# A head's output squared in PSUM and scaled on its way out by ScalarE, in a one-core hybrid encoder layer

## The chip, the cores and the metric

One core of one Trainium2 chip runs the whole layer in one launch. The metric is the device time of that launch in microseconds (us). The kernel before takes 1037.61 us, the median of 3 runs (1036.9 to 1039.13).

## The reference

The layer has 512 tokens of width 1024. One projection of x gives the inputs of two branches and two gates; the part that matters here is the branch of gated delta rules, with 8 heads of width 128 and a forward and a backward pass.

```python
proj = x @ w_in[l]
qkv, z, a, bb, sc_b, sc_c, sc_x, gate_a, gate_b = _split_in(proj)
...
o = o_fwd + o_bwd
zf = z.astype(jnp.float32).reshape(bsz, t, N_HEADS, HEAD_DIM)
o = (o * lax.rsqrt(jnp.mean(jnp.square(o), axis=-1, keepdims=True) + RMS_EPS)
     * norm_w.astype(jnp.float32) * jax.nn.silu(zf))
return o.reshape(bsz, t, GDN_WIDTH).astype(out_dtype) @ w_o
...
mixed = jax.nn.sigmoid(gate_a) * y_a + jax.nn.sigmoid(gate_b) * y_b
x = _layer_norm(DEEPNORM_ALPHA * x + mixed @ w_out[l], ln1_g[l], ln1_b[l])
h = jnp.square(jax.nn.relu(x @ w_up[l] + b_up[l]))
x = _layer_norm(DEEPNORM_ALPHA * x + h @ w_down[l] + b_down[l], ln2_g[l], ln2_b[l])
```

The change is in the middle statement: for each head and token, the sum of squares of the output o, the inverse root of it, and the product of o with that root.

## The kernel before

All large products run in three passes: each float32 operand is split into a high part, made by a ScalarE copy, and a low part, made by a VectorE subtraction (`split`, `split_w`), and TensorE adds high times high, high times low and low times high (lines 158 to 160). A block of projection is 8 steps (`KT`) of three 128x512 matmuls, in `proj_steps`; its weights come by DMA, are split some steps ahead, and stand in two buffers.

The heads' own work is small against that and is woven into the stream of projection blocks. Nine slots (`h` from 0 to 8, line 777) each run some blocks; a slot has `L` steps, 8 times the number of its blocks. By `REST` and the three blocks of the next head's keys, queries and values, slots 1 to 5 have 48 steps, slots 6 and 7 have 40, and slot 8 has 8. At each step `u` of slot `h` up to three generators are advanced by one piece: `new`, the local part of head h + 1; `mid`, the rest of the local part of head h, which inverts a triangular matrix by blocks; and `far`, the scan over chunks and the end of head h - 1. Tables say at which steps: `FAR` for `far`, `MID` for `mid`, `BEGIN` for `new`.

```python
for _ in range(FAR.count(u) if far else 0):
    step(far)
...
for g in (mid, far) if h < NH else ():
    if g:
        run(g)
```

An entry of a table that is not below the slot's `L` is never met in the loop; what is left of `mid` and then of `far` is run at once when the slot is over (the second loop above, line 801). Inside these slots the order written here is the order of the instructions on TensorE, VectorE, ScalarE and GpSimd (`manual_schedule`), and each engine takes its list in order. The last head's `far` runs on beside the next stage's blocks (line 820 and after), every third step.

The scan (`gdn_scan`) adds both directions of a head's output into one PSUM bank, `po`, tag "o", of which there is one buffer; the next head's scan writes the same bank. At the scan's end, ScalarE copies `po` (128 tokens x 4 chunks x 128) to `ot` in SBUF (line 687). Then `gdn_end` has three pieces. In the first ScalarE squares `ot` chunk by chunk and sums each token's row into `so` (line 695). In the second VectorE and GpSimd make the inverse root `ro` of `so` by three Newton steps (`rsqrt`, whose tile is `nryo`; it ends with line 425), and GpSimd multiplies `ot` by it (line 699). In the third TensorE transposes the four chunks into `pot` (line 703) and ScalarE copies that to `on`, scaled by the norm's weight (line 704).

Other names: `pyb` is the last product of the block inversion in `mid` (line 615), which VectorE (line 619) and ScalarE (line 621) copy into `na`; `dg` (line 507) and `vt` (line 526) are copies of `new`; `kd` (line 650) is a 128x128 copy from SBUF scaled by token, `vh` (line 668) a 128x128 copy from PSUM; `px`, `lx` and `py` (lines 574 to 583) are an earlier step of the inversion; `wh_in` (line 124) is the high part of a block's weights, `ps_in` and `ps_osc` are banks of projection blocks.

Of the kernel before, what the change touches and what calls it, by code (L numbers as in the profile page):

```python
# [8 lines left out]
F32 = mybir.dt.float32  # L9
F32R = mybir.dt.float32r  # L10
I32 = mybir.dt.int32
AF = mybir.ActivationFunctionType
ALU = mybir.AluOpType
AX = mybir.AxisListType

P = 128
# [4 lines left out]
NCH = 4  # L21
# [18 lines left out]
KEYS1 = 31  # L40
MID = (0, 2, 15, 19, 24, 25, 27, 29, 30, 33, 36, 40)
MID0 = (23, 23, 34, 49, 56, 56, 58, 59, 60, 64, 70, 92)
FAR = (0, 4, 8, 10, 13, 13, 14, 14, 14, 14, 15, 15, 20, 25, 30, 31, 48)
SPLIT_AT = (3, 2)
LOW_AFTER = (3, 5)
CONV = ((0, 1, 3), (0, 1, 3), (0, 0, 3), (5, 3, 4))
# [15 lines left out]
def kernel(  # L62
# [25 lines left out]
    nc = tc.nc  # L88
    act = nc.scalar.activation
# [11 lines left out]
    def ps(kind, name, shape=(P, NT)):  # L101
        return psum.tile(list(shape), F32, tag=kind, name=name, bufs={"m": 2, "g": 2, "l": 1, "s": 2, "o": 1}[kind])
# [143 lines left out]
    gdn = tc.alloc_tile_pool(name="gdn", bufs=1, side="right")  # L246
# [49 lines left out]
    for d in range(2):  # L296
        stt(out=gg[:, d], in0=pl[:, :, 8 * d:8 * d + 8], scalar=-1.0,
            in1=ea[:, 8 * d:8 * d + 8].unsqueeze(1).broadcast_to([P, NCH, 8]), op0=ALU.mult, op1=ALU.mult)
# [47 lines left out]
    for g in range(2):  # L346
        for t in range(2):
            nc.sync.dma_start(out=eye.rearrange("(b g) (s t) j -> g t b s j", g=2, t=2)[g, t],
                              in_=diag[2 * t + g, 0:4, 0:16].partition_broadcast(P // 2))
# [63 lines left out]
    def rsqrt(v, name):  # L413

        eng = nc.gpsimd if RS_POOL else nc.vector
        y = gdn.tile([P, NCH], F32, tag=f"nry{name[0]}", name=f"nry{name}", bufs=2)
        t = gdn.tile([P, NCH], F32, tag=f"nrt{name[0]}", name=f"nrt{name}", bufs=2)
        nc.vector.tensor_scalar(out=t.bitcast(I32), in0=v.bitcast(I32), scalar1=1, scalar2=None, op0=ALU.logical_shift_right)
        nc.vector.tensor_scalar(out=y.bitcast(I32), in0=t.bitcast(I32), scalar1=-1.0, scalar2=float(0x5F3759DF),
                                op0=ALU.mult, op1=ALU.add)  # L420
        for _ in range(3):
            eng.tensor_tensor(out=t, in0=y, in1=y, op=ALU.mult)
            eng.tensor_tensor(out=t, in0=t, in1=v, op=ALU.mult)
            eng.tensor_scalar(out=t, in0=t, scalar1=-0.5, scalar2=1.5, op0=ALU.mult, op1=ALU.add)
            eng.tensor_tensor(out=y, in0=t, in1=y, op=ALU.mult)
        return y
# [213 lines left out]
    def gdn_scan(h, qk, kt, vt, W, AT, qd, nbk, ss):  # L640
        po = ps("o", f"po{h}")
        S = [None, None]
        first = True
        for i in range(NCH):
            chunk = (i, NCH - 1 - i)
            kds = []
            if i != NCH - 1:
                for d, c in enumerate(chunk):
                    kd = gdn.tile([P, P], F32, tag="kd", name=f"kd{h}_{d}_{c}", bufs=4)
                    act(out=kd, in_=kt[:, c, :], func=AF.Copy, scale=nbk[:, d, c:c + 1])  # L650
                    kds.append(kd)
                yield
            pcs, vhs, Rs = [], [], []
            for d, c in enumerate(chunk):
                pcs.append(ps("s", f"pc{h}_{d}_{c}"))
                Rs.append(vt[:, c, :])
            if i:
                for d, c in enumerate(chunk):
                    nc.tensor.matmul(pcs[d][:, 0:P], qk[:, 0, c * P:(c + 1) * P], S[d], start=True, stop=True)
                    Rs[d] = gdn.tile([P, P], F32, tag="R", name=f"R{h}_{d}_{c}", bufs=2)  # L660
                    stt(out=Rs[d], in0=pcs[d][:, 0:P], scalar=egc[:, d, c, h:h + 1], in1=vt[:, c, :], op0=ALU.mult, op1=ALU.add)
                for d, c in enumerate(chunk):
                    nc.tensor.matmul(po[:, c * P:(c + 1) * P], qd[:, d, c, :], S[d], start=False, stop=False, skip_group_check=True)
                yield
            for d, c in enumerate(chunk):
                nc.tensor.matmul(pcs[d][:, P:2 * P], W[:, d, c, :], Rs[d], start=True, stop=True)  # L666
                vh = gdn.tile([P, P], F32, tag="vh", name=f"vh{h}_{d}_{c}", bufs=4)
                act(out=vh, in_=pcs[d][:, P:2 * P], func=AF.Copy)
                vhs.append(vh)
            yield  # L670
            if i != NCH - 1:
                for d, c in enumerate(chunk):
                    ds = pcs[d][:, 2 * P:3 * P]
                    nc.tensor.matmul(ds, kds[d], vhs[d], start=True, stop=True)
                    Sn = gdn.tile([P, P], F32, tag="S", name=f"S{h}_{d}_{c}", bufs=4)
                    if i == 0:
                        act(out=Sn, in_=ds, func=AF.Copy)
                    else:
                        stt(out=Sn, in0=S[d], scalar=egl[:, d, c, h:h + 1], in1=ds, op0=ALU.mult, op1=ALU.add)
                    S[d] = Sn  # L680
            for d, c in enumerate(chunk):
                nc.tensor.matmul(po[:, c * P:(c + 1) * P], AT[:, d, c, :], vhs[d], start=first, stop=False, skip_group_check=True)
                first = False
            if i != NCH - 1:
                yield
        ot = gdn.tile([P, NCH, P], F32, tag="ot", name=f"ot{h}", bufs=1)
        act(out=ot.rearrange("p c d -> p (c d)"), in_=po, func=AF.Copy)
        return h, ss, ot

    def gdn_end(h, ss, ot):  # L690

        so = gdn.tile([P, NCH], F32, tag="so", name=f"so{h}", bufs=2)
        sqj = gdn.tile([P, P], F32, tag="sqo", name=f"sqo{h}", bufs=1)
        for c in range(NCH):
            act(out=sqj, in_=ot[:, c, :], func=AF.Square, accum_out=so[:, c:c + 1])
        yield
        stt(out=so, in0=ss[:, 1, :], scalar=128.0 * 128.0 * 1e-6, in1=so, op0=ALU.mult, op1=ALU.add)
        ro = rsqrt(so, f"o{h}")
        nc.gpsimd.tensor_tensor(out=ot, in0=ot, in1=ro.unsqueeze(2).broadcast_to([P, NCH, P]), op=ALU.mult)
        yield  # L700
        pt = ps("s", f"pot{h}")
        for c in range(NCH):
            nc.tensor.transpose(pt[:, c * P:(c + 1) * P], ot[:, c, :], ident)
        act(out=on[h], in_=pt, func=AF.Copy, scale=nwn)
        made.add(("on", h))
# [49 lines left out]
    def scan_end(h):  # L755
        done = yield from gdn_scan(*state[h])
        yield
        yield from gdn_end(*done)
# [6 lines left out]
    def step(g):  # L765
        try:
            next(g)
            return True
        except StopIteration:
            return False  # L770
# [3 lines left out]
    with tc.manual_schedule(engines=MANUAL):  # L774
        clock[0] = 0
        mid = local(0)
        for h in range(NH + 1):
# [5 lines left out]
            for u in range(L):  # L783
                if h == 0:
                    if u == KEYS0:
                        run(gdn_keys(0))
                    for _ in range(BEGIN0.count(u)):
                        step(mid)
                for _ in range(FAR.count(u) if far else 0):
                    step(far)  # L790
# [28 lines left out]
    yb = []  # L819
    left = len(FAR) - 1 - sum(u < KT * REST[NH] for u in FAR)  # L820
    for c in range(8):
# [266 lines left out]
```

## Time and profile before

| | |
|---|---|
| median of 3 runs | 1037.61 us (1036.9 to 1039.13) |
| the profiled execution | 1038.9 us |
| its span | 1037.2 us |
| its mean granted TensorE clock | 0.994 |
| TensorE matmuls busy | 1024.6 us (99%), 6611 |
| VectorE busy | 509.1 us (49%) |
| ScalarE busy | 451.1 us (43%) |
| GpSimd busy | 282.9 us (27%) |

The span is the time from the first to the last instruction of the profiled execution; the execution's own time is 1.7 us longer. PE is TensorE's matmuls, DVE VectorE, ACT ScalarE and POOL GpSimd. The granted clock is given as a share of full speed: 1.00 is 2.4 GHz, 0.50 is 1.2 GHz. Matmuls are pipelined, so their durations overlap: the distance between two starts, not the duration, is what each costs.

### The profile page before, as it was taken

To read this page: it belongs to the slowest core of one execution; us is meant where nothing else is said; L and a number is where in the kernel's file an instruction comes from. 1 tells how busy PE (TensorE), PEld (TensorE's weight loads), DVE (VectorE), ACT (ScalarE), POOL (GpSimd) and SP (SyncE) were. 2 spreads that over 40 slices of the span, in tenths; PEclk is the share of its full clock that TensorE was granted. 3 is DMA by queue.
4 is the path that set the end of the run, shared out by engine and by line. 5 is a ranking of instruction groups with operands and counts; after the bars stand their busy time and mean duration, and the time that the engine had idled before them with its cause. 6 is when DMAs were issued, how large, how long until landed. Compare 5 with 4: busy or idle time off the path is not lost.

```text
span 1037.2 us, 16574 instructions
## 1 busy us (share of the span) xinstructions
PE 1024.6 (99%) x6611; PEld 852.7 (82%) x6611; DVE 509.1 (49%) x923; ACT 451.1 (43%) x823; POOL 282.9 (27%) x524
## 2 busy tenths in 40 slices
PE   9999999999999999999999999999999999999997
PEld 7777878888888888888888888898888888888885
DVE  6856566767676675442422274761222143333336
ACT  5853657475757564453424232332233243232231
POOL 0070525262534436411230021003752220000002
PEclk9998999999999999999999999999999999999999
DMA  6413322332323322322335334232332342333312
GB/s 223 144 35 112 99 73 58 102 88 85 99 76 89 90 51 70 89 82 82 102 112 213 102 97 133 96 101 82 100 86 100 102 142 82 102 101 94 95 55 82
DMA packets 57238, 101.80 MB, mean 98 GB/s; under 512 B 30728, under 2 KB 32200, under 8 KB 57160
## 3 DMA queue, kind: packets, MB, share of 16 engines
q1 hardware_dynamic: 56440, 99.42, 31.8%
q8 instruction: 52, 0.85, 0.3%
q10 hardware_dynamic: 720, 1.31, 0.3%
q14 instruction: 26, 0.21, 0.1%
HBM read 97.27 MB, written 3.44 MB: 97 GB/s over the span
## 4 chain that ended last, share of the span: by engine, by line
PE 94%; DVE 2%; POOL 2%; DMA 1%; ACT 1%; issue 1%; SPq 0%; DVEq 0%; POOLq 0%; ACTq 0%
PE accd L904 17%; PE ps_in L158 12%; PE ps_in L160 12%; PE ps_in L159 12%; PE ps_up L159 5%; PE ps_up L158 5%; PE ps_up L160 5%; PE acco L904 4%; PE psup L954 2%; PE pc L666 1%; PE ps_osc L158 1%; PE ps_osc L160 1%; PE ps_osc L159 1%; PE ps_ogd L159 1%; PE ps_ogd L158 1%; PE ps_ogd L160 1%
## 5 line engine op out<-in xcount | busy, mean ns | idle before, releaser
L158 PE MATMUL ps_in<-xh,wh_in 128*128 128x512 f32 x576 | 236.7, 411 | 0.0
L160 PE MATMUL ps_in<-xh,wl_in 128*128 128x512 f32 x576 | 226.8, 394 | 0.0
L159 PE MATMUL ps_in<-xl,wh_in 128*128 128x512 f32 x576 | 226.6, 393 | 0.0
L160 PEld LDWEIGHTS ps_in<-xh,wl_in 128*128 128x128 f32 x576 | 109.1, 189 | 24.3
L120 DVE TENSOR_TENSOR wl_in<-raw_in,wh_in 128x1024 fp32r<-128x1024 f32 x70 | 92.5, 1322 | 73.3 <-ACT wh_in L124 73.1
L158 PEld LDWEIGHTS ps_in<-xh,wh_in 128*128 128x128 f32 x576 | 109.3, 190 | 21.4 <-ACT xh L105 0.5
L159 PEld LDWEIGHTS ps_in<-xl,wh_in 128*128 128x128 f32 x576 | 109.4, 190 | 19.2 <-issue 0.3
L124 ACT ACTIVATE wh_in<-raw_in 128x1024 fp32r<-128x1024 f32 x70 | 73.9, 1056 | 66.6 <-PE ps_in L159 56.3
L904 PE MATMUL accd<-wh_down,hh 128*128 128x512 f32 x256 | 99.6, 390 | 0.0
L904 PE MATMUL accd<-wh_down,hl 128*128 128x512 f32 x256 | 99.4, 389 | 0.0
L904 PE MATMUL accd<-wl_down,hh 128*128 128x512 f32 x256 | 99.4, 389 | 0.0
L120 DVE TENSOR_TENSOR wl_up<-raw_up,wh_up 128x1024 fp32r<-128x1024 f32 x30 | 36.8, 1225 | 121.4 <-ACT wh_up L124 121.4
L961 POOL TENSOR_TENSOR hf<-r 128x512 f32<-128x512 f32 x32 | 46.3, 1446 | 156.2 <-ACT r L959 156.2
L158 PE MATMUL ps_up<-x1h,wh_up 128*128 128x512 f32 x224 | 87.1, 389 | 0.0
L159 PE MATMUL ps_up<-x1l,wh_up 128*128 128x512 f32 x224 | 87.1, 389 | 0.0
L160 PE MATMUL ps_up<-x1h,wl_up 128*128 128x512 f32 x224 | 87.1, 389 | 0.0
L124 ACT ACTIVATE wh_up<-raw_up 128x1024 fp32r<-128x1024 f32 x30 | 31.8, 1060 | 105.7 <-PE ps_up L159 98.1
L106 DVE TENSOR_TENSOR wl_down<-raw_down,wh_down 128x1024 fp32r<-128x1024 f32 x32 | 39.1, 1225 | 51.5 <-ACT wh_down L105 50.1
L904 PEld LDWEIGHTS accd<-wh_down,hh 128*128 128x128 f32 x256 | 48.0, 188 | 10.3 <-ACT wh_down L105 0.4
L904 PEld LDWEIGHTS accd<-wh_down,hl 128*128 128x128 f32 x256 | 48.1, 188 | 10.1
L904 PEld LDWEIGHTS accd<-wl_down,hh 128*128 128x128 f32 x256 | 48.0, 188 | 9.9
L105 ACT ACTIVATE wh_down<-raw_down 128x1024 fp32r<-128x1024 f32 x32 | 33.6, 1053 | 49.7 <-PE accd L904 49.7
(271 smaller groups left out, 1829.8 us busy)
## 6 DMA issues: line engine op xcount, KB each, us to landing
raw_in<-in_w_in SPq DMA_DIRECT2D x70, 512.0 KB, 3.7
raw_up<-in_w_up SPq DMA_DIRECT2D x32, 512.0 KB, 3.5
raw_down<-in_w_down SPq DMA_DIRECT2D x32, 512.0 KB, 3.6
grow<-gcd SPq DMA_DIRECT2D x8, 512.0 KB, 4.8
raw_osc<-in_w_o_sc SPq DMA_DIRECT2D x8, 512.0 KB, 3.6
raw_ogd<-in_w_o_gdn SPq DMA_DIRECT2D x8, 512.0 KB, 3.6
raw_out<-in_w_out SPq DMA_DIRECT2D x8, 512.0 KB, 3.6
xr<-in_xT SPq DMA_DIRECT2D x8, 256.0 KB, 5.3
```

What stands on the lines that cost most here:

```text
L105: act(out=hi, in_=src, func=AF.Copy)
L106: (lo_eng or nc.vector).tensor_tensor(out=lo, in0=src, in1=hi.bitcast(F32), op=ALU.subtract)
L120: (nc.gpsimd if pool else nc.vector).tensor_tensor(out=wl, in0=raw, in1=wh.bitcast(F32), op=ALU.subtract)
L124: act(out=wh, in_=raw, func=AF.Copy)
L158: nc.tensor.matmul(acc, wh[:, c], mh[k], start=(k == 0), stop=False)
L159: nc.tensor.matmul(acc, wh[:, c], ml[k], start=False, stop=False)
L160: nc.tensor.matmul(acc, wl[:, c], mh[k], start=False, stop=(k == KT - 1))
L666: nc.tensor.matmul(pcs[d][:, P:2 * P], W[:, d, c, :], Rs[d], start=True, stop=True)
L904: nc.tensor.matmul(acc[:, o], a[:, ts_], b[:, hs], start=start and j == 0, stop=stop and j == 2, skip_group_check=True)
L954: nc.tensor.matmul(acc[:, ts_], a[:, c], b[k][:, ts_], start=(k == 0 and t2 == 0 and j == 0), stop=(k == KT - 1 and t2 == 1 and j == 2), s ...
L961: square = nc.gpsimd.tensor_tensor(out=hfl, in0=r, in1=r, op=ALU.mult)
```

## The change

The copy of `po` to `ot` goes. ScalarE squares straight from `po`, four instructions as before. The multiply on GpSimd goes too; in its place ScalarE makes `ot` with four copies of 128x128 from `po`, each scaled by that chunk's column of `ro`. These copies are a piece of their own in `gdn_end`, so a head's `far` has 18 pieces instead of 17, and `FAR` has a new entry, 44. The bank `po` is released by the last of the scaled copies instead of by the copy. In the changed kernel line numbers behind the edit are one higher.

```diff
-FAR = (0, 4, 8, 10, 13, 13, 14, 14, 14, 14, 15, 15, 20, 25, 30, 31, 48)
+FAR = (0, 4, 8, 10, 13, 13, 14, 14, 14, 14, 15, 15, 20, 25, 30, 31, 44, 48)
...
-        ot = gdn.tile([P, NCH, P], F32, tag="ot", name=f"ot{h}", bufs=1)
-        act(out=ot.rearrange("p c d -> p (c d)"), in_=po, func=AF.Copy)
-        return h, ss, ot
-
-    def gdn_end(h, ss, ot):
+        return h, ss, po
+
+    def gdn_end(h, ss, po):
...
-            act(out=sqj, in_=ot[:, c, :], func=AF.Square, accum_out=so[:, c:c + 1])
+            act(out=sqj, in_=po[:, c * P:(c + 1) * P], func=AF.Square, accum_out=so[:, c:c + 1])
         yield
         stt(out=so, in0=ss[:, 1, :], scalar=128.0 * 128.0 * 1e-6, in1=so, op0=ALU.mult, op1=ALU.add)
         ro = rsqrt(so, f"o{h}")
-        nc.gpsimd.tensor_tensor(out=ot, in0=ot, in1=ro.unsqueeze(2).broadcast_to([P, NCH, P]), op=ALU.mult)
+        yield
+        ot = gdn.tile([P, NCH, P], F32, tag="ot", name=f"ot{h}", bufs=1)
+        for c in range(NCH):
+            act(out=ot[:, c, :], in_=po[:, c * P:(c + 1) * P], func=AF.Copy, scale=ro[:, c:c + 1])
         yield
```

TensorE's list is the same in both kernels. Its piece where slot 6 ends and head 5 with it, in the changed kernel; the words in brackets name the engine that an instruction waits for, and the numbers behind the names count tiles:

```order
L615 MATMUL pyb_4939<-na_4039,lxb_4872 64x64 [waits DVE_49]
L615 MATMUL pyb_4939<-na_4039,lxb_4872 64x64 x7
L704 MATMUL pot_4955<-ident,ot_4950 128x128 [waits Activation_49] x4
L158 MATMUL ps_in_4979<-xh_73,wh_in_4842 128x512
L159 MATMUL ps_in_4979<-xl_81,wh_in_4842 128x512
```

In the kernel before, the first of these four transposes waits for GpSimd and the other three for nothing; here each waits for ScalarE.

ScalarE's list at the same place, before:

```order
L526 ACTIVATE vt_4896<-pv_4891 128x512
L712 ACTIVATE zt_4930<-ps_in_4791 128x512
L621 ACTIVATE na_4031<-pyb_4932 64x4x64
L704 ACTIVATE on_199<-pot_4943,nwn 128x512
L650 ACTIVATE kd_0_0_4950<-kt_3902,nbk_3943 128x128
```

and with the change:

```order
L526 ACTIVATE vt_4903<-pv_4898 128x512
L713 ACTIVATE zt_4937<-ps_in_4798 128x512
L621 ACTIVATE na_4039<-pyb_4939 64x4x64
L700 ACTIVATE ot_4950<-po_4361,nryo_4779 128x128 x4
L705 ACTIVATE on_199<-pot_4955,nwn 128x512
L650 ACTIVATE kd_0_0_4962<-kt_3910,nbk_3951 128x128
```

The four scaled copies come in between the copy of `pyb` and that of `pot`. At the end of slot 7, with head 6, both lists have the same sequence.

ScalarE's list in slot 1, with head 0, whose `L` is 48, with the change:

```order
L621 ACTIVATE na_798<-pyb_1702 64x4x64
L124 ACTIVATE wh_in_1733<-raw_in_1509 128x1024
L700 ACTIVATE ot_1753<-po_1196,nryo_1614 128x128 x4
L507 ACTIVATE dg_1764<-na_1507 32x128 x4
L526 ACTIVATE vt_1787<-pv_1782 128x512
L705 ACTIVATE on_194<-pot_1823,nwn 128x512
```

Here they stand four rows ahead of the copy of `pot`, behind a weight split.

## Rows read from the trace of the kernel before

**Rows 1.** The page, part 1: busy us, share of the span and instructions of each engine.

```profile
PE 1024.6 (99%) x6611; PEld 852.7 (82%) x6611; DVE 509.1 (49%) x923; ACT 451.1 (43%) x823; POOL 282.9 (27%) x524
```

**Rows 2.** PE's waits, whole span: us in total, times, longest.

```profile
PE px L574 <- DVE UT L567: 2.1, 1, 2.1
...
PE pv L524 <- DVE na L498: 1.0, 1, 1.0
```

**Rows 3.** One stretch: busy us of PE and matmuls, granted clock, DMA share, GB/s.

```profile
100.00:1020.00 920.00, 920.00 (x5962) 1.00 0.32 94
```

**Rows 4.** Instructions on ot and on (ScalarE): ns min/median/max, first and last start.

```profile
L687 ACT ACTIVATE ot<-po x8: 597/597/598, 136.3 to 484.2; 128x512 f32<-128x512 f32 x8
...
L704 ACT ACTIVATE on<-pot,nwn x8: 682/687/689, 159.0 to 541.2; 128x512 f32<-128x512 f32 x8
```

**Rows 5.** Timeline, one turn of a slot of 48 steps: start us, us.

```profile
293.44 0.20 POOL L425 TENSOR_TENSOR nryo<-nrto,nryo 128x4 f32<-128x4 f32 x1
...
298.39 1.06 ACT L124 ACTIVATE wh_in<-raw_in 128x1024 fp32r<-128x1024 f32 x1
...
301.69 0.31 ACT L507 ACTIVATE dg<-na 32x128 f32<-32x128 f32 x1 [2.24 <-DVE na L498]
...
305.82 0.60 PE L703 MATMUL pot<-ident,ot 128*128 128x128 f32 x4
```

**Rows 6.** Timeline, the end of head 7.

```profile
490.78 1.06 ACT L124 ACTIVATE wh_in<-raw_in 128x1024 fp32r<-128x1024 f32 x1 [2.97 <-PE ps_osc L159]
...
491.56 0.20 POOL L425 TENSOR_TENSOR nryo<-nrto,nryo 128x4 f32<-128x4 f32 x1
...
496.25 0.39 PE L158 MATMUL ps_in<-xh,wh_in 128*128 128x512 f32 x1
```

**Rows 7.** Timeline, ScalarE and VectorE where heads 5 and 6 end.

```profile
398.66 0.42 DVE L619 COPY na<-pyb 64x256 f32<-64x256 f32 x1 [0.54 <-PE pyb L615]
...
399.11 0.38 ACT L621 ACTIVATE na<-pyb 64x256 f32<-64x256 f32 x1 [0.47 <-DVE na L619]
...
399.52 0.69 ACT L704 ACTIVATE on<-pot,nwn 128x512 f32<-128x512 f32 x1
...
400.10 0.68 ACT L650 ACTIVATE kd<-kt,nbk 128x128 f32<-128x128 f32 x2
...
402.21 0.50 ACT L668 ACTIVATE vh<-pc 128x128 f32<-128x128 f32 x2 [0.48 <-PE pc L666]
...
440.15 0.69 ACT L704 ACTIVATE on<-pot,nwn 128x512 f32<-128x512 f32 x1
```

**Rows 8.** ScalarE by line and shape: busy us, mean ns.

```profile
L650 ACT ACTIVATE kd<-kt,nbk 128x128 f32<-128x128 f32 x48 | 16.6, 397 | 0.0
...
L668 ACT ACTIVATE vh<-pc 128x128 f32<-128x128 f32 x64 | 16.0, 274 | 30.7 <-PE pc L666 29.9
```

**Rows 9.** Timeline, from a ScalarE end to the product that waits for it.

```profile
80.17 0.38 ACT L576 ACTIVATE lx<-px 128x256 f32<-128x256 f32 x1 [2.57 <-PE px L574]
...
80.61 1.08 PE L583 MATMUL py<-U,lx 32*32 32x32 f32 x64 [0.49 <-ACT lx L576]
```

**Rows 10.** Timeline, PE at the transposes of heads 5 and 6.

```profile
398.55 0.66 PE L703 MATMUL pot<-ident,ot 128*128 128x128 f32 x4
...
398.96 0.48 PE L158 MATMUL ps_in<-xh,wh_in 128*128 128x512 f32 x1
...
405.46 0.61 PE L682 MATMUL po<-vh,na 128*128 128x128 f32 x4
...
438.91 0.66 PE L703 MATMUL pot<-ident,ot 128*128 128x128 f32 x4
...
439.32 0.48 PE L158 MATMUL ps_in<-xh,wh_in 128*128 128x512 f32 x1
```

**Rows 11.** PE's granted clock behind two waits, columns as in rows 3.

```profile
51.00:56.00 5.00, 5.00 (x17) 0.66 0.14 19
...
79.00:86.00 7.00, 6.48 (x166) 0.52 0.57 195
```

## The prediction

> **What bounds the kernel now.** I read the page first, then the waits of TensorE, then stretches of the timeline. The page's busy line has TensorE matmuls busy 1024.6 us of 1037.2, the others at half of that or less [rows 1]. That line alone can hide waits, so the next view is the list of what PE waited for. Its two longest waits are 2.1 and 1.0 us, for VectorE [rows 2], and both lie in the first 100 us, just ahead of the stretches of [rows 11]. From 100 to 1020 us PE is busy every microsecond at a granted clock of 1.00, the higher level, 2.4 GHz [rows 3]. The edit works on eight heads; the copy that it removes first stands at 136 us, and the last instruction that follows from it, the copy on of head 7, at 541 us [rows 4]. So in the stretch that it touches PE never waits: no engine made faster there can give anything back, and any wait put in front of PE is paid in full.
>
> **What is removed and added, engine by engine.** GpSimd loses eight multiplies of ot. ScalarE loses eight copies of a 128x512 bank and gains 32 scaled copies of 128x128. The squares stay, reading PSUM instead of SBUF. TensorE's list stays the same instruction for instruction; only the engine that its eight groups of transposes wait for changes, from GpSimd to ScalarE. As nothing waits for GpSimd or for the removed copy in this stretch, their removal is worth 0: the cover is PE's own stream of projections. What remains is where the new copies stand in ScalarE's queue, which goes in order, and the heads fall into three kinds.
>
> *Heads 0 to 4.* Their slots have 48 steps, so the entry 44 of FAR is reached. The four copies stand behind a weight split and ahead of the copies to dg. In the trace the split ends at 299.45 us and ScalarE then idles 2.24 us until 301.69 [rows 5]. GpSimd's last Newton step on the scale starts at 293.44 us and takes 0.20, so the scale is there almost 6 us earlier [rows 5]. The four copies take 1.23 us (below), which fits in the gap with 1.0 us left. PE's transposes of that head come at 305.82 us [rows 5], 5 us after the copies would end at 300.7. Cost 0; if the gap were gone, the dg copies would be late by about a microsecond.
>
> *Head 7.* In the stretch after the slots the copies come ahead of the split that ran at 490.78 us and wait for GpSimd, whose last step there starts at 491.56 us [rows 6]. With four squares done together GpSimd starts a little earlier, but the split behind it may be late by up to 1.2 us. The block that needs these weights starts at 496.25 us [rows 6], over 3 us later than the split would end. Cost 0.
>
> *Heads 5 and 6.* Their ends lie in slots of 40 steps, so neither 44 nor 48 is reached and both last steps are run one right after the other when the slot is over. PE's list has the inversion's last product (pyb), then the four transposes (pot), then the next projection. Until now the transposes found ot long since scaled. Now they wait for ScalarE, and ScalarE cannot start early: the copies stand behind its copy of pyb into na (L621), which itself waits for VectorE's copy (L619), which waits for pyb on PE [rows 7]. So the wait is built into the order of the two lists.
>
> **The price of one wait.** No row of before is a 128x128 copy from PSUM with a per-token scale. Without a scale (vh) one takes 0.274 us [rows 8] and a pair 0.50 [rows 7], a step of 0.226, so four take 0.95. With a scale but from SBUF (kd) one takes 0.397 [rows 8] and a pair 0.68 [rows 7], a step of 0.29, so four take 1.26. These are the ends. Of two 128x512 copies from PSUM the one with a per-partition scale (on) takes 0.687, the one without (ot) 0.597 [rows 4], so the scale adds 0.09 and one copy is 0.36; with kd's step four take 1.23. I take 1.23, as kd shares the scale.
>
> Head 5: ScalarE is free of L621 and starts its next instruction at 399.52 us [rows 7]; the four end at 400.75. From a ScalarE end to the product that waits for it takes 0.06 us: lx starts at 80.17 and lasts 0.38, py starts at 80.61 [rows 9]. The four transposes took 0.41 us from their start to the next projection (398.55 to 398.96 [rows 10]); three now run between the copies, and the last one with its own weight load costs 0.10 to 0.24, say 0.2. The projection resumes at 401.0 instead of 398.96: **2.05 us**. With 0.95 and 0.10 it is 1.67, with 1.26 and 0.24 it is 2.1.
>
> Head 6: ScalarE's next instruction starts at 440.15 us [rows 7], so the projection resumes at 440.15 + 1.23 + 0.06 + 0.2 = 441.64 instead of 439.32 [rows 10]: **2.3 us**, between 1.95 and 2.4.
>
> Together 4.35 us, between 3.6 and 4.5. Behind these waits ScalarE's own list (on, kd, weight splits) is late by about as much as PE, so no third wait arises. The bank po is held until the copies end at 400.75; the next head first writes it at 405.46 [rows 10].
>
> **The clock.** The two longest waits of before were each followed by a fall of the granted clock to 0.5, the lower level, 1.2 GHz. After the 2.1 us wait for UT it was low from 79 to beyond 85 us, mean 0.52 over 7 us; after the wait for na of 1.0 us, followed by small products, mean 0.66 over 5 us [rows 11]. Lost: 0.48 x 7 = 3.4 us in the first, where PE also idled between two small products; 0.34 x 5 = 1.7 us in the second, where dense work came at once. The new waits are 2 us long with small products on both sides and dense work behind, so each may cost nothing or about 1.7 us; the second row is nearer. In its section "Why this matters for your kernels" the Trainium skill's page "TensorE: Matmul & The Clock Gate" has the clock fall only after an idle gap longer than either of these waits. By that rule no clock is lost and the sum stays 4.35; the row after the 2.1 us wait speaks against it, and the measurement decides.
>
> **Sum.** 4.35 for the waits and 1.7 for one fall: 6.05. The profiled execution took 1038.9 us, 1.7 more than its span, so it would take 1044.95. It is 1.3 above the median of the three runs, 1037.61, which becomes **1043.7**.
>
> **Rivals.**
> *No fall of the clock.* Both waits come and the clock stays at 1.00: 1037.61 + 4.35 = 1042.0. For it: the transposes break the idle time up, the longest piece being the wait for the first copy, 1.3 us (from about 398.6 to 399.52 + 0.36 + 0.06). Against it: both waits that come near in length were followed by a fall. It is what the Trainium skill's rule named above would give.
> *Two falls.* 4.35 + 3.4: 1045.4. For it: the two places are alike. Against it: a fall after the shorter wait needed more than the wait itself, so whether one comes looks like chance.
> *Not slower.* PE does not stand still at the transposes: it would go on with the projection behind them, which waits for nothing new, and take the transposes up when ot is there. Price 0, 1037.6; it decides if PE can pass over a matmul that waits. The Trainium skill (same page, "Architectural detail") says PE's queue may pull weight loads ahead of matmuls in flight, which is less than that. Against it: PE stood for 2.1 us at px [rows 2] with projections behind it in its list.
> *The change does nothing.* Excluded by the lists: the squares read po, and the multiply is gone from GpSimd's.
> *Faster* has no room: PE waits nowhere after 100 us.
>
> **How the numbers follow.** One fall 0.45 (1043.7), no fall 0.25 (1042.0), two falls 0.22 (1045.4), not slower 0.06, anything else 0.02. About 0.2%, 2.1 us, is what a measurement tells from no change; the first three cases lie at 3.6 us and more. So slower 0.92, same 0.06, faster 0.02. The range runs from no fall with the cheap copies, 1037.61 + 3.6 = 1041.2, to two falls with the dear ones and 0.3 of spread between runs, 1037.61 + 4.5 + 3.4 + 0.3 = 1045.8.
>
> **What would show it.** In the trace after, PE waits for ScalarE's ot at the transposes twice, 1.7 to 2.4 us in all each (in up to four pieces), near 398 and 441 us, and nowhere else; the granted clock of the few microseconds behind each says which case it is. The four copies take 0.95 to 1.26 us. GpSimd's busy time falls, ScalarE's grows, and neither shows in the time. I would be wrong if the two waits are missing, if heads 0 to 4 wait too, or if a wait appears at the first write of po.

## The result, and the profile after

The changed kernel takes 1043.49 us, the median of 4 runs (1042.94 to 1044.82), against 1037.75 us of before in 4 runs: a ratio of 1.0052 with a 95% interval of 1.004 to 1.0064, so it is slower by 4.2 to 6.6 us. Its profiled execution took 1042.94 us with a span of 1041.2.

The page's first part shows the engines as they were to move: against [rows 1] GpSimd's busy time fell by 13.6 us and ScalarE's rose by 3.6, and TensorE works as much as before in a longer span.

```profile
PE 1024.1 (98%) x6611; PEld 850.9 (82%) x6611; DVE 507.8 (49%) x923; ACT 454.7 (44%) x847; POOL 269.3 (26%) x516
```

The waits of TensorE over the whole span of the changed kernel (us in total, times, longest), to be held against [rows 2]:

```profile
PE px L574 <- DVE UT L567: 3.1, 1, 3.1
PE pot L704 <- ACT ot L700: 2.9, 2, 1.6
PE warm L187 <- DVE epsl L241: 1.1, 1, 1.1
PE pv L524 <- DVE na L498: 1.0, 1, 1.0
```

Behind 110 us there is one new line: the transposes wait for ScalarE's ot, twice. The longer wait at px lies ahead of that, and by the first pyb the two traces are level again (108.90 us before, 108.99 after). The 2.9 us are the waits for the first copy of each group only; the gaps between the four transposes come on top. TensorE's timeline at the two places (start us, us) shows the whole of it:

```profile
398.07 0.68 PE L615 MATMUL pyb<-na,lxb 64*64 64x64 f32 x16
400.08 1.11 PE L704 MATMUL pot<-ident,ot 128*128 128x128 f32 x4 [1.32 <-ACT ot L700]
400.94 0.47 PE L158 MATMUL ps_in<-xh,wh_in 128*128 128x512 f32 x1
...
440.29 0.68 PE L615 MATMUL pyb<-na,lxb 64*64 64x64 f32 x16
442.56 1.10 PE L704 MATMUL pot<-ident,ot 128*128 128x128 f32 x4 [1.59 <-ACT ot L700]
443.42 0.48 PE L158 MATMUL ps_in<-xh,wh_in 128*128 128x512 f32 x1
```

From pyb to the next projection it is 2.87 us at head 5 and 3.13 us at head 6. In the trace of before pyb started at 397.93 and 438.29 us and the projections of [rows 10] 1.03 us later at both places. The waits cost 1.84 and 2.10 us, together 3.94. ScalarE's timeline at head 5 gives the reason, to be held against [rows 7]:

```profile
399.25 0.38 ACT L621 ACTIVATE na<-pyb 64x256 f32<-64x256 f32 x1 [0.47 <-DVE na L619]
399.65 1.15 ACT L700 ACTIVATE ot<-po,nryo 128x128 f32<-128x128 f32 x4
401.22 0.69 ACT L705 ACTIVATE on<-pot,nwn 128x512 f32<-128x512 f32 x1 [0.42 <-PE pot L704]
```

ScalarE first copies pyb, which TensorE has just made, then takes 1.15 us for the four scaled copies, and TensorE stands meanwhile. Heads 0 to 4 are as forecast: at head 3 the copies fill the gap of [rows 5] and TensorE's transposes come 5 us later.

```profile
298.49 1.06 ACT L124 ACTIVATE wh_in<-raw_in 128x1024 fp32r<-128x1024 f32 x1
299.58 1.15 ACT L700 ACTIVATE ot<-po,nryo 128x128 f32<-128x128 f32 x4
301.79 1.26 ACT L507 ACTIVATE dg<-na 32x128 f32<-32x128 f32 x4 [1.07 <-DVE na L498]
...
305.92 0.60 PE L704 MATMUL pot<-ident,ot 128*128 128x128 f32 x4
```

At head 7 ScalarE does wait for GpSimd, 3.4 us, with a weight split behind it ([rows 6] before), and no wait of TensorE comes of it:

```profile
494.69 1.15 ACT L700 ACTIVATE ot<-po,nryo 128x128 f32<-128x128 f32 x4 [3.40 <-POOL nryo L425]
495.70 1.07 ACT L124 ACTIVATE wh_in<-raw_in 128x1024 fp32r<-128x1024 f32 x1
```

The two profiled executions differ by 4.0 us of span, about the 3.94. The medians differ by 5.74; the profiled execution is the fastest of the changed kernel's four. The granted clock in the stretches behind the two waits (us busy, granted clock, DMA share, GB/s) shows none of the fall that I had put into the sum:

```profile
398.00:402.00 4.00, 2.68 (x26) 1.00 0.61 166
402.00:408.00 6.00, 6.00 (x34) 1.00 0.31 94
440.00:452.00 12.00, 10.41 (x64) 1.00 0.25 79
```

So two things were to be tested: whether the two waits are the whole cause, and what makes the medians differ by more than the traces.

### The profile page after: what moved, and what is told of

Its sections match the earlier page's. It is cut to its first block, busy times and chain, and to the rows that moved or that the text cites. A ratio compares the mean times of both kernels' runs of the same rounds, so it can differ in the third digit from the quotient of the medians.

```text
span 1041.2 us, 16581 instructions
## 1 busy us (share of the span) xinstructions
PE 1024.1 (98%) x6611; PEld 850.9 (82%) x6611; DVE 507.8 (49%) x923; ACT 454.7 (44%) x847; POOL 269.3 (26%) x516
## 4 chain that ended last, share of the span: by engine, by line
PE 93%; DVE 2%; POOL 2%; ACT 1%; DMA 1%; issue 1%; SPq 0%; DVEq 0%; POOLq 0%; ACTq 0%
PE accd L905 17%; PE ps_in L158 12%; PE ps_in L160 12%; PE ps_in L159 11%; PE ps_up L158 5%; PE ps_up L159 5%; PE ps_up L160 5%; PE acco L905 4%; PE psup L955 2%; PE pc L666 1%; PE ps_osc L158 1%; PE ps_osc L160 1%; PE ps_ogd L158 1%; PE ps_ogd L159 1%; PE ps_osc L159 1%; PE ps_ogd L160 1%
## 5 line engine op out<-in xcount | busy, mean ns | idle before, releaser
L105 ACT ACTIVATE wh_down<-raw_down 128x1024 fp32r<-128x1024 f32 x32 | 33.7, 1053 | 49.8 <-PE accd L905 49.8
```

The source lines that it names most:

```text
L105: act(out=hi, in_=src, func=AF.Copy)
```

## The experiments

**Copies early in all slots.** FAR's entry 44 becomes 38, which slots of 40 steps reach too.

```diff
-FAR = (0, 4, 8, 10, 13, 13, 14, 14, 14, 14, 15, 15, 20, 25, 30, 31, 44, 48)
+FAR = (0, 4, 8, 10, 13, 13, 14, 14, 14, 14, 15, 15, 20, 25, 30, 31, 38, 48)
```

> The changed kernel with FAR's entry 44 turned into 38, which every slot reaches, those of 40 steps too, so that heads 5 and 6 have their scaled copies ahead of the copy of pyb. If the two waits at the transposes are the cause of the whole loss, they are gone and the time is that of the kernel before, 1037 to 1038.5 us. If reading PSUM four times, the longer hold of po or the added ScalarE work costs something in itself, it stays 2 us or more above before.

1038.32 us (11 runs) against 1037.88 of before in the same job (15 runs): a ratio of 1.0005, 0.9996 to 1.0014. TensorE's list of waits has no pot in it. In ScalarE's timeline at head 5 the copies now stand ahead of the copy of pyb, with three rows between:

```profile
394.38 1.14 ACT L700 ACTIVATE ot<-po,nryo 128x128 f32<-128x128 f32 x4
395.39 1.25 ACT L507 ACTIVATE dg<-na 32x128 f32<-32x128 f32 x4
...
399.50 0.38 ACT L621 ACTIVATE na<-pyb 64x256 f32<-64x256 f32 x1 [0.47 <-DVE na L619]
```

All of the change's operations are there, and nothing is left of the loss that could be told from none. The two waits, with what comes behind them, are the cause; the squares in PSUM, the held bank and the added ScalarE work cost at most 1.5 us by the interval, and nothing that could be measured.

**Copies late in all slots.** The entry 44 becomes 48, so that every head has them directly ahead of the copy of pot.

```diff
-FAR = (0, 4, 8, 10, 13, 13, 14, 14, 14, 14, 15, 15, 20, 25, 30, 31, 44, 48)
+FAR = (0, 4, 8, 10, 13, 13, 14, 14, 14, 14, 15, 15, 20, 25, 30, 31, 48, 48)
```

> The changed kernel with FAR's entry 44 turned into 48, so that in all slots the copies stand right ahead of the copy of pot, as at heads 5 and 6. If the wait comes from standing behind the copy of pyb, heads 0 to 4 have none (their pyb lies 8 steps earlier and ScalarE is idle for 2 us ahead of the transposes): two waits as before, 1043 to 1044 us. If copies that stand right ahead of the transposes always stop TensorE for about 2 us, there are seven waits and about 1053 us.

1044.09 us (4 runs), ratio 1.0062 (1.0048 to 1.0076), and again two waits at pot, not seven:

```profile
PE pot L704 <- ACT ot L700: 2.9, 2, 1.6
```

At heads 0 to 4 ScalarE makes the copies before TensorE comes to the transposes: at head 3 they ran from 303.31 to 304.46 us and the transposes began at 304.77. Standing directly ahead of them costs nothing; standing behind the copy of pyb does. This trace also caught what the others had missed, a fall of the clock behind head 6's wait:

```profile
441.00:442.00 1.00, 0.61 (x3) 0.96 0.00 0
442.00:443.00 1.00, 1.00 (x4) 0.50 0.69 102
443.00:444.00 1.00, 1.00 (x4) 0.50 0.81 311
444.00:445.00 1.00, 1.00 (x4) 0.50 0.28 111
445.00:446.00 1.00, 1.00 (x5) 0.84 0.00 0
```

From pyb to the next head's first write of po it took 13.10 us here (439.12 to 452.22), 11.66 in the changed kernel's trace (440.29 to 451.95): the fall cost 1.44 us.

**The two waits filled.** Seven extra 128x512 matmuls stand ahead of the transposes of heads 5 and 6; their result is overwritten.

```diff
         pt = ps("s", f"pot{h}")
+        for _ in range(7 if h in (5, 6) else 0):
+            nc.tensor.matmul(pt, xh[0][:, :P], xh[1], start=True, stop=True)
```

> The changed kernel with seven extra 128x512 matmuls into pot ahead of the transposes of heads 5 and 6 (7 x 0.227 = 1.6 us, shorter than the wait, their result is overwritten), so that TensorE is busy in most of the wait. If the median's loss is 3.9 us of waits and the rest is lower clock behind them, the rest goes and the time is 1041.5 to 1042. If the rest is something else, it is that of the changed kernel run again in the same job.

1043.25 us (1041.34 to 1043.96, 5 runs), above the 1041.5 to 1042 that was to be expected if the rest were falls of the clock. In its trace TensorE is busy all the time at 1.00 from 110 to 1020 us.

**The changed kernel again.** It was run beside the filled one.

> The changed kernel again, unedited, for its spread and a second trace. If some of the executions lose clock behind the two waits, the median is again about 5.7 us above before, its executions fall into groups about 1.7 us apart, and one of the traces shows 0.5 behind a wait. If the 1.8 us above the two waits was chance in the first 100 us of the programs, the median is about 3.9 us above before, 1041.7.

1043.52 us (1041.07 to 1044.83, 5 runs), ratio 1.0058 (1.0045 to 1.0072). So the 5.7 us of the medians came again, but the executions do not fall into groups 1.7 us apart, and its trace showed no fall either. The traced execution is the fastest of the five; its span is 1.9 us shorter than in the first trace because its start is (first pyb at 106.82 us, against 108.99). The pair does not settle what the rest is: the filling gained 0.3 us, where 1.8 was looked for, between two samples that spread over 2.6 and 3.8 us, and the mean granted clock did not rise with it (0.9948 filled, 0.9952 bare, means of five). Two waits are too few to see what lies behind them, so the next pair has seven.

**Seven waits, bare and filled.** In slots of 48 steps the copies and the transposes run straight behind pyb as well, which gives heads 0 to 4 the same wait.

```diff
-FAR = (0, 4, 8, 10, 13, 13, 14, 14, 14, 14, 15, 15, 20, 25, 30, 31, 44, 48)
+FAR = (0, 4, 8, 10, 13, 13, 14, 14, 14, 14, 15, 15, 20, 25, 30, 31, 48, 48)
...
+                if far and L == 48 and u == 40:
+                    step(far)
+                    step(far)
```

> The changed kernel in which the slots of 40 steps are as they were and the slots of 48 steps run the copies and the transposes straight behind pyb, in step 40, so that heads 0 to 4 get the same wait as heads 5 and 6. Seven waits of about 1.95 us: 13.7 us above before, 1051.6, if a wait costs what the two traces of the changed kernel show and no more. If behind a wait the clock also falls in a share p of the cases for 1.4 us, it is 7 x 1.4 x p more: 1056.5 at p = 0.5, 1061 at p = 1, and the trace shows 0.5 behind some of the seven.

1055.4 us (1054.99 to 1056.88, 4 runs), 16.9 above this job's before (1038.51). With the same seven extra matmuls ahead of the transposes of heads 0 to 6:

> As the run with seven waits, and each of the seven filled with seven extra 128x512 matmuls into pot whose result is overwritten, shorter than the wait. If falls of the clock behind the waits make up what is above 13.7 us, they go with the filling: 1051.6, clock 1.00 from 110 to 1020 us. If the filling does nothing, it is as with seven unfilled waits.

1051.14 us (1049.98 to 1052.23, 4 runs), 12.6 above before. The stand itself is the same in both: at head 1 from pyb to the next projection 2.86 us bare (199.77 to 202.63) and 2.86 filled (199.36 to 202.22), and at the other six heads they agree to 0.01 us. Yet the filled kernel is faster by 4.26 us, and the runs' ranges lie 2.8 us apart. Over the stretch from 110 to 1020 us of the filled kernel TensorE is busy all the time at 1.00:

```profile
110.00:1020.00 910.00, 910.00 (x5891) 1.00 0.31 94
```

In the bare one the trace has one fall, again behind head 6:

```profile
443.00:460.00 17.00, 15.41 (x119) 0.90 0.31 93
```

That fall is not the whole difference of the two traces, whose spans lie 4.0 us apart. From head 6's pyb to the end, with the fall, the bare one takes 1.5 us longer (450.84 to 1053.3 against 448.37 to 1049.3). Two more gaps of TensorE, away from the transposes and missing from the filled trace, make it later by 2.1 us. For the first the profile shows nothing that TensorE waited for, the second waited for VectorE's UT; whether they come of the bare waits or by chance, one trace does not tell:

```profile
239.24 0.26 PE L583 MATMUL py<-U,lx 32*32 32x32 f32 x6 [0.98 <-issue]
...
390.58 0.74 PE L574 MATMUL px<-UT,dg 32*32 32x32 f32 x64 [0.81 <-DVE UT L567]
```

The remaining 0.4 us had come about by the first pyb (108.29 us bare, 107.92 filled), ahead of the first of the seven waits.

The mean granted clock of each run points the same way as the times: 0.994, 0.992, 0.991 and 0.993 bare, 0.997, 0.997, 0.995 and 0.997 filled. Means of 0.9925 and 0.9965 over 1053 and 1049 us are 7.9 and 3.7 us of lost clock. But they count the falls of the whole program. In the two traces a good part of the difference lies ahead of all the waits; first the bare one, then the filled one (length, us busy, granted clock, DMA share, GB/s):

```profile
75.00:90.00 15.00, 11.43 (x220) 0.77 0.46 128
...
75.00:90.00 15.00, 11.40 (x226) 0.89 0.44 128
```

These are 3.4 and 1.7 us of lost clock, a difference as large as the 1.7 us of the fall behind head 6. So it is shown that the filling gained 4.26 us, and not how much of it was clock. By the traces one fall behind seven waits is 1.5 / 7 = 0.2 us per wait; by the medians it is 4.26 / 7 = 0.6 if nothing else made the difference. In the four traces with bare waits of about 2 us (the changed kernel twice, the copies late, the seven waits) two of thirteen waits have a fall behind them.

**GpSimd's multiply, late.** The kernel before, with only the change's table: the multiply becomes a piece of its own at 44.

```diff
         ro = rsqrt(so, f"o{h}")
+        yield
         nc.gpsimd.tensor_tensor(out=ot, in0=ot, in1=ro.unsqueeze(2).broadcast_to([P, NCH, P]), op=ALU.mult)
```

> The kernel before (copy of po, multiply by GpSimd) with the change's table alone: the multiply is a piece of its own at entry 44. If the engine is what costs, this is as before, 1037.9. If the place in the engine's list is, head 5 waits for GpSimd, whose list has a long run of small work ahead of the multiply there (until about 402.6 us in the trace of before, then 1 us for the multiply): about 4.8 us at head 5, none at head 6, 1042.7, or 1044 with a fall of the clock.

1044.92 us (4 runs), ratio 1.0057 (1.004 to 1.0074). One wait, at head 5, with the clock low behind it:

```profile
PE pot L704 <- POOL ot L700: 5.1, 1, 5.1
```

```profile
400.00:413.00 13.00, 9.99 (x40) 0.74 0.21 65
```

ScalarE has no part in this. That the loss is as large is chance: it is one wait of 5.1 us and a longer fall, where the changed kernel has two waits of 2 us. What costs is the late place in an engine's ordered list in a slot of 40 steps, on GpSimd as on ScalarE.

**Copies directly behind the Newton steps.** The entry 31 twice, without 44.

```diff
-FAR = (0, 4, 8, 10, 13, 13, 14, 14, 14, 14, 15, 15, 20, 25, 30, 31, 44, 48)
+FAR = (0, 4, 8, 10, 13, 13, 14, 14, 14, 14, 15, 15, 20, 25, 30, 31, 31, 48)
```

> The changed kernel with the copies straight behind the Newton steps' issue, entry 31 twice instead of 31 and 44. ScalarE would wait for GpSimd's Newton steps with the inversion's copies (L621) behind it: about 3.5 us at pxb in each of seven heads, 1062, and up to 1072 with falls of the clock. If ScalarE's waits don't reach TensorE, 1038.

1068.22 us (one run, so no interval), inside the 1062 to 1072 that were expected. The wait moved to pxb, which VectorE's and ScalarE's inversion copies feed; the second row is ScalarE's own wait:

```profile
PE pxb L603 <- DVE mt L635: 18.8, 7, 3.4
...
ACT ot L700 <- POOL nryo L425: 31.5, 8, 4.0
```

Seven waits of 2.7 us on average, where 3.5 was expected, and in the trace a fall of the clock to 0.50 behind four of them; the mean clock is 0.987. Too early costs more than too late: ScalarE then waits for GpSimd with the inversion behind it.

## Why the prediction was right

**Heads 0 to 4 and 7 at no cost:** right, by the timelines above.

**The two waits:** right in place, cause and number; each was put a little too high. The four copies took 1.15 us, not 1.23 (one copy took 0.368, estimated at 0.36, but the step to the next was 0.26, between kd's 0.29 and vh's 0.226). From the last copy's end, 400.80, the projection resumed after 0.14 us; I had put 0.26, of which 0.2 for the last transpose, chosen between 0.10 and 0.24. So 1.84 for 2.05 and 2.10 for 2.32, together 3.94 for 4.35, inside the bounds of 3.6 to 4.5.

**The clock:** that a fall can follow such a wait was right, and a fall that was caught cost 1.44 us against 1.7. One fall per execution is not borne out. The traces have a fall behind two of thirteen such waits; with 0.2 to 0.6 us per wait from the seven-wait pair, two waits lose 0.4 to 1.2 us, by chance from one execution to the next. The 1.7 was taken from the fall behind the wait of 1.0 us for na; the same wait stands in the changed kernel's first trace with a clock of 1.00 from 50 to 70 us. Nor is that wait the second longest: there is one of 1.1 us at warm, ahead of the program's first matmul, and no fall comes behind it. The Trainium skill's page "TensorE: Matmul & The Clock Gate", section "Why this matters for your kernels", has the clock fall only after longer gaps than these; the trace of the copies late, with 0.50 behind a first gap of 1.6 us, does not agree with it, and the measurement decides.

**The sum:** 3.94 and 0.4 to 1.2, so 4.3 to 5.1 us by the runs, 6.05 by the prediction, 5.74 by the medians, whose interval is 4.2 to 6.6. Both terms of the prediction were too large, so that the total came within 0.3 us of the medians is in part luck. What makes up the 0.6 to 1.4 us that the runs leave stays open: it lies within the interval, the start of the program alone differs by 2 us between the two traces of the changed kernel, and both traces are the fastest executions of their sets. The rival without a fall, 1042.0, describes the two traced executions, but the medians lie above it.

**The rivals:** that TensorE might pass over the waiting transposes is refuted by its timeline. That the engine or the PSUM reads cost something is refuted by the copies at 38, and for the engine also by the late GpSimd multiply.

## What to carry to other kernels

When one engine is busy all the time and the others are woven around it by a table, an edit's cost is not its work but the place of its instructions in each engine's ordered list: ask at every place where the table's entry falls, also in the shorter slots that never reach it. A step that ends up behind a copy of what the busy engine has just made, and ahead of what it does next, is a wait by construction, and its length can be read off beforehand from the two lists and one trace. Add to it what the clock may lose behind the wait; here that was between 0.2 and 0.6 us on average for each wait of 2 us.

## What the runs showed of the hardware that I had not expected

Filling waits with matmuls whose result is overwritten made the kernel faster when there were seven of them: stands of the same length cost 12.6 us with 49 extra matmuls in them and 16.9 without. Part of this is the granted clock, 0.50 behind one of the seven bare waits and 1.00 behind all the filled ones; how large a part is not shown. With two waits filled no gain could be told from noise (1043.25 us against 1043.52).

Whether the clock falls behind one and the same wait changes from one execution to the next: behind the 1.0 us wait for na it had a mean of 0.66 over 5 us in the trace of the kernel before ([rows 11]) and 1.00 in the first trace of the changed one.
